# GpSimd's elementwise work to VectorE and ScalarE in a two-layer attention trunk

## The chip, the cores and the metric

The kernel runs on one core of one Trainium2 chip. The metric is the device time of one execution in microseconds (us); the median of several executions is compared. In the profile PE is TensorE (its matmuls), PEld its weight loads, DVE is VectorE, ACT is ScalarE, POOL is GpSimd and SP is SyncE, whose queue issues loads.

## The reference

One batch of 512 tokens of width 1024 goes through two layers, each with a residual and an RMS norm before and after. Layer A is multi-head latent attention (8 heads), layer B differential attention (8 heads); both have a SiLU gate.

```python
def mla_layer(h, ...):                       # layer A
    u = rmsnorm(h, pre_g); c_q, c_kv, k_r, z = split(u @ w_in)
    q = rmsnorm(c_q) @ w_uq                  # per head 128 plain + 64 with rope
    c_kv = rmsnorm(c_kv); k_n, v = c_kv @ w_uk, c_kv @ w_uv
    p = masked_softmax((q_n k_n + rope(q_r) rope(k_r)) * scale)
    return h + rmsnorm(((p v) * silu(z)) @ w_o, post_g)

# the shared K/V of layer B come from h once: k = rope(k), v = u @ w_kv
def diff_layer(h, ...):                      # layer B
    q, z = split(rmsnorm(h) @ w_in); q = rope(q)   # q1, q2 of 64 each
    p = masked_softmax(q1 k1 * scale) - lam * masked_softmax(q2 k2 * scale)
    o = rmsnorm(p v, subln_g) * (1 - lam_init)
    return h + rmsnorm((o * silu(z)) @ w_o, post_g)
```

The mask is chunk-causal: a query block of 128 sees the keys up to its own chunk of 64.

## The kernel before, in words

Every matmul is made of three: each operand is split into a rounded high part and the rest, and `mm3` (L187 to L191) adds high by high, high by low and low by high into PSUM. Activations lie transposed, features on the partitions and the 512 tokens along the row, so most elementwise instructions are 128x512.

**Weights.** `Stream` (L63) holds the weights in their order of use. For each unit SP's queue loads the raw tile `wr` (L89). For the first units `wh` and `wl` are made by VectorE (L104, L107, L137 and L138); from L365 on `ws.cast` is true: the high part `wh` comes by a second, rounding transfer on GpSimd's queue (L112), and VectorE makes `wl` as raw minus high (L113). `ahead` keeps two units ahead of PE, in three buffers.

**Stages.** The start (L336 to L364) runs over eight blocks of x: ScalarE scales x into `xh` (L338) and squares it (L347), VectorE makes `xl` (L339), the squares are added up in `acc_x` (L349), and PE makes five projections `g`. Then `trig` (L320) makes sine and cosine tables, VectorE for the angles (L322 to L328) and ScalarE for the values (L329 to L331); the tables for layer A are `CA` and `SA`, for layer B `CB` and `SB`. `cq` (L391) makes six projections and adds their squares in `acc_q` (L400); `acc_kv` (L413) does so for `g`. Between the second and the third `cq` PE adds `acc_x` and `acc_kv` over the partitions (L421 to L430, tiles `ssx` and `sskv`), which needs their split by ScalarE and VectorE (`axh`, `axl`, `akh`, `akl`).

Layer A then goes through its heads in the order `aorder`, layer B in `border` (L250): projections k, q and z of later heads stand between the scores (s), transposes (t) and the product with v (p) of earlier ones. In layer B `proj_b` makes k and q: PE's projection, `rope` (L375: a shuffle, two products and a sum: L378, L379, L380, L381), ScalarE's halves (L836, L840), and VectorE's rests (L838 for q, L841 for k). `scores_b` is four matmuls for each of four query blocks (L872, L875), then `softmax_part` (L522 on VectorE, L525 on ScalarE); the second softmax, times lambda over its sum, is scaled (L883, tile `ec`) and subtracted (L884, tile `eb`), in four pieces of 128, 256, 384 and 512 columns. `transposes` turns the result on PE and splits it (`pth` on ScalarE, `ptl` on VectorE, L133 and L138). After the product with v, `subln` scales the gate by the head's norm (L910 to L912).

Between the layers `chain_a` (L717) normalises each of four token tiles, stores the rows (L722), and scales them into h (L723); PE transposes h (`trans_h`, L735), and VectorE and ScalarE evacuate it (`evac_h`, L742 to L745). In `vb_half0` (L753) the first projections of layer B, `vb_0` to `vb_3`, stand between the transposes of tiles 2 and 3.

**Order.** A scheduler of the framework decides, when the kernel is built, in which order the instructions stand on each engine, from its own model of their times; each engine then runs its list strictly in order, waiting for semaphores. Only in `wo_end` and `vb_half0` PE's order is that of the program (`pe_order`). So an edit that changes where one operation runs can change the order of others on every engine.

Of the kernel before, what the change touches and what calls it, by code (L numbers as in the profile page):

```python
# [15 lines left out]
AF = mybir.ActivationFunctionType  # L16
ALU = mybir.AluOpType
# [41 lines left out]
def f(ap):  # L59
    return ap.bitcast(F32)  # L60
# [80 lines left out]
def body(tc, ins, outs, dbg=None):  # L141
    nc = tc.nc
    ctx = ExitStack()
    with ctx:
        _body(ctx, tc, nc, ins, outs, dbg or {})


def _body(ctx, tc, nc, ins, out, dbg):
    pool = lambda name, bufs, **k: ctx.enter_context(tc.tile_pool(name=name, bufs=bufs, **k))
# [13 lines left out]
    act, dve, gps, pe = nc.scalar, nc.vector, nc.gpsimd, nc.tensor  # L163

    def ps(name):
        return psp.tile([P, 512], F32, tag="ps", name=name)

    def big_t(name, dt=F32R):
        return big.tile([P, 8, 512], dt, tag="big", name=name)

    def hd_t(name, dt=F32R):
        return hd.tile([P, 512], dt, tag="hd", name=name)

    def tmp_t(name, dt=F32):
        return tmp.tile([P, 512], dt, tag="tmp", name=name)

    def tab_t(name):
        return tmp.tile([P, 512], F32, tag="tmp", name=name)

    def sm_t(name, n=4, bufs=None):  # L180
        return sm.tile([P, n], F32, tag=name, name=name, bufs=bufs)
# [5 lines left out]
    def mm3(o, w, x, first, last):  # L187

        pe.matmul(o, w[0], x[0], start=first, stop=False)  # L189
        pe.matmul(o, w[0], x[1], start=False, stop=False)  # L190
        pe.matmul(o, w[1], x[0], start=False, stop=last)  # L191
# [20 lines left out]
    def add_wo(src):  # L212
        def second(p):
            ws.add(src[1, p], lambda which, k:
                   w1[which][:, 2 * p:2 * p + 2].rearrange("p a b -> p (a b)") if w1 else None)
        for p in range(3):
            ws.add(src[0, p])
            second(p)
        second(3)
        ws.add(src[0, 3])  # L220

    ws = Stream(nc, wrp, whp, wlp)
# [32 lines left out]
    border = [(nm, h) for nm, h in border if h < H]  # L255
    for nm, h in border:
        if nm in "kqz":
            ws.add(ins[f"w_{nm}b"][h], None, None if nm == "q" else ("pool", "pool"))
    add_wo(ins["w_ob"])

    wraw = big_t("wraw", F32).rearrange("p a b -> p (a b)")
# [30 lines left out]
    def col(c):  # L292
        return cols[:, c:c + 1]
# [19 lines left out]
    acc_x = hd_t("acc_x", F32)  # L313
# [22 lines left out]
    for kc in range(KC):  # L336
        for c in first if kc == 0 else [slice(0, 512)]:
            behind = act.activation(xh[:, kc, c], xr[:, kc, c], AF.Copy, scale=col(C_PRE + kc))  # L338
        dve.scalar_tensor_tensor(xl[:, kc], xr[:, kc], col(C_PRE + kc), f(xh[:, kc]),  # L339
                                 op0=ALU.mult, op1=ALU.subtract)  # L340
        g = [ws.get()]
        if kc == 0:
            g.append(ws.get())
        ws.ahead(3 if kc == 0 else 2)
        sq = acc_x if kc == 0 else hd_t("sqx", F32)
        with tc.issue_after(behind.ins):
            act.activation(sq, xr[:, kc], AF.Square)  # L347
        if kc:
            gps.tensor_tensor(acc_x, acc_x, sq, op=ALU.add)  # L349
        for m in range(5):  # L350
            gh, gl = g[1 if kc == 0 and m else 0]
            k = m - 1 if kc == 0 and m else m
            ms = slice(k * P, k * P + P)
            if kc == 0 and m == 0:
                for c in first:
                    pe.matmul(g0[m][:, c], gh[:, 0, ms], xh[:, kc, c], start=c is first[0], stop=False)
                pe.matmul(g0[m], gl[:, 0, ms], xh[:, kc], start=False, stop=False)
                pe.matmul(g0[m], gh[:, 0, ms], xl[:, kc], start=False, stop=False)
                continue
            if m == 4:  # L360
                for part in (xh, xl):
                    pe.matmul(g0[m], gh[:, 0, ms], part[:, kc], start=kc == 0 and part is xh, stop=kc == 7 and part is xl)
                continue
            mm3(g0[m], (gh[:, 0, ms], gl[:, 0, ms]), (xh[:, kc], xl[:, kc]), kc == 0, kc == 7)  # L364
# [10 lines left out]
    def rope(src, C, Sn, shuf):  # L375

        a, b = tmp_t("ra"), tmp_t("rb")
        dve.stream_shuffle(b, src, shuf)  # L378
        dve.tensor_tensor(a, src, C, op=ALU.mult)  # L379
        gps.tensor_tensor(b, b, Sn, op=ALU.mult)  # L380
        dve.tensor_tensor(a, a, b, op=ALU.add)  # L381
        return a

# [4 lines left out]
    acc_q, acc_kv, rx = hd_t("acc_q", F32), hd_t("acc_kv", F32), tab_t("rx")  # L388
    xe_col = sm_t("xe_col", 4, 1)

    def cq(m):  # L391
        wh, wl = ws.get()
        o = ps(f"cq{m}")
        for kc in range(KC):
            mm3(o, (wh[:, kc], wl[:, kc]), (xh[:, kc], xl[:, kc]), kc == 0, kc == KC - 1)
        act.activation(cqh[:, m], o, AF.Copy, scale=col(C_Q + m))
        sq = acc_q if m == 0 else tmp_t("sq")
        act.activation(sq, o, AF.Square)
        if m:
            gps.tensor_tensor(acc_q, acc_q, sq, op=ALU.add)  # L400
        dve.scalar_tensor_tensor(cql[:, m], o, col(C_Q + m), f(cqh[:, m]), op0=ALU.mult, op1=ALU.subtract)
        ws.ahead()

# [5 lines left out]
    for m in range(4):  # L409
        sq = acc_kv if m == 0 else hd_t("sqkv", F32)  # L410
        act.activation(sq, g0[m], AF.Square)
        if m:
            gps.tensor_tensor(acc_kv, acc_kv, sq, op=ALU.add)  # L413
    axh, axl = tmp_t("axh", F32R), tmp_t("axl", F32R)
    split(nc, axh, axl, acc_x)
    akh, akl = hd_t("akh"), hd_t("akl")
    split(nc, akh, akl, acc_kv)
    cq(0)
    cq(1)
    ssx = ps("ssx")  # L420
# [25 lines left out]
    zg = big_t("za", F32)  # L446
# [174 lines left out]
    v3 = lambda a: a.rearrange("p (k t) -> p k t", k=4)  # L621
# [4 lines left out]
    def post(parts, done=None):  # L626

        r = sm_t("r", 1)
        inv_norm(r, [o for o, _, _, _ in parts], [j3(tmp_t("sq"), o) for o, _, _, _ in parts])
        for o, g, _, t in parts:  # L630
            dve.tensor_tensor(t, o, g, op=ALU.mult)
        for n, (_, _, res, t) in enumerate(parts):
            dve.scalar_tensor_tensor(res, t, r, res, op0=ALU.mult, op1=ALU.add)
            if done:
                done(n)
# [79 lines left out]
    def chain_a(i, o1):  # L715
        res = xrows[i]
        ts = [hTf[:, 4 * n:4 * n + 4, i * P:i * P + P] for n in range(2)]  # L717
        post([(v3(o), v3(g), v3(x), t) for o, g, x, t in zip((st["acc"][i], o1), g_a, res, ts)])
        r = sm_t("rh", 1)
        inv_norm(r, [v3(a) for a in res], ts)  # L720
        for n in range(2):
            gps.dma_start(hdr[i, n], res[n])  # L722
            gps.tensor_scalar(ts[n], v3(res[n]), r, 1.0, op0=ALU.mult, op1=ALU.mult)  # L723
        hrows[i] = ts

    gkv_b = cols[:, C_BKV:C_BKV + 8]
# [76 lines left out]
    for p in range(4):  # L803
        wh, wl = ws.get()
        for kc in (2 * p, 2 * p + 1):
            act.activation(hT2h[:, kc], hTf[:, kc], AF.Copy, scale=col(C_BPRE + kc))
            dve.scalar_tensor_tensor(hT2l[:, kc], hTf[:, kc], col(C_BPRE + kc), f(hT2h[:, kc]),
                                     op0=ALU.mult, op1=ALU.subtract)
# [10 lines left out]
    zg = big_t("zb", F32)  # L819
# [41 lines left out]
    def scores_b(h):  # L861
        (kb, kl), (qb, _) = qkb.pop(("k", h)), qkb.pop(("q", h))
        second = {}

        def src(i):


            n = P * (i + 1)
            ti = slice(i * P, i * P + P)
            os = [ps(f"sb{h}_{g}_{i}") for g in range(2)]  # L870
            for g in range(2):
                pe.matmul(os[g][:, :n], qb[g][:, ti], kb[g][:, :n], start=True, stop=False)  # L872
            for g in range(2):
                rs = slice(64 * g, 64 * g + 64)
                pe.matmul(os[g][:, :n], qb[g][rs, ti], kl[rs, :n], start=False, stop=True)  # L875
            second[i] = os[1]
            return os[0]

        (e1, r1), (e2, r2) = softmax_part(h, "bc", [src, second.get], -SCALE_B)
        dve.tensor_scalar(r2, r2, lam_c, None, op0=ALU.mult)  # L880
        for i in range(NT):
            w = slice(OFF[i], OFF[i] + P * (i + 1))
            gps.tensor_scalar(e2[:, w], e2[:, w], r2[:, i:i + 1], 1.0, op0=ALU.mult, op1=ALU.mult)  # L883
            dve.scalar_tensor_tensor(e1[:, w], e1[:, w], r1[:, i:i + 1], e2[:, w],  # L884
                                     op0=ALU.mult, op1=ALU.subtract)
        es[h] = e1
# [19 lines left out]
    def subln(h):  # L906
        b = ps(f"ssb{h}")
        pe.matmul(b, ones_r if h < H - 1 else ones, ob.pop(h), start=True, stop=True)
        rs = tmp_t("rs")
        act.activation(rs, b, AF.Ln, bias=eps_c, scale=1.0 / 128)  # L910
        act.activation(rs, rs, AF.Exp, scale=-0.5)
        (dve if h > 4 else gps).tensor_tensor(zg[:, h], zg[:, h], rs, op=ALU.mult)  # L912

    def after_b(h, o):
        subln_sq(h, o)
# [101 lines left out]
```

## Time and profile before

| | us |
|---|---|
| median of 3 executions | 608.12 (607.16 to 609.12) |
| the profiled execution | 609.05 |
| its span in the trace | 607.0 |
| PE busy | 589.6 |
| DVE busy | 420.1 |
| ACT busy | 255.0 |
| POOL busy | 158.8 |

The span is what the trace covers; the execution's own time is 2.05 us longer. Busy times of engines overlap. PE's share is 97% of the span, so what PE does not do in the span is 17.4 us; a part of its busy time is at half clock. A row of a timeline gives the start, the duration, the engine, the line, what is written and read, and in brackets for how long the engine had been idle and what ended that.

### The profile page before, as it was taken

What the parts mean: (1) busy time and instruction counts of PE and PEld (TensorE: products, weight loads), DVE (VectorE), ACT (ScalarE), POOL (GpSimd) and SP (SyncE); (2) the same over time, 40 slices, a digit from 0 to 9 for tenths busy, and PEclk for the clock granted to TensorE, in tenths of its full rate; (3) what the DMA queues carried; (4) which work ended last, traced back from release to release, by engine and by line L of the source; (5) the groups of instructions that cost most, each with busy time, mean ns of one, the idle gap of its engine ahead of it and who ended that gap; (6) DMA issues with size and microseconds to landing.
All of it is one profiled execution on the core that took longest, in us unless ns stands there. A gap on an engine that the chain in (4) does not pass through costs nothing.

```text
span 607.0 us, 7782 instructions
## 1 busy us (share of the span) xinstructions
PE 589.6 (97%) x2742; PEld 481.4 (79%) x2742; DVE 420.1 (69%) x806; ACT 255.0 (42%) x560; POOL 158.8 (26%) x216
## 2 busy tenths in 40 slices
PE   7999999999999999999999999999997999999995
PEld 6786888888888888888888887878776677687885
DVE  6997852345576666756876458847999688988654
ACT  6046311122334444421664125245664539647431
POOL 5232610112232323321440112405325134242000
PEclk9998999999999999999999999999999699799999
DMA  8155555555552426787431656464244142269302
GB/s 305 43 157 191 157 190 208 183 164 140 170 147 91 135 91 207 239 326 268 165 106 47 245 174 202 138 209 138 83 129 137 52 157 76 99 194 357 110 35 105
DMA packets 32215, 96.61 MB, mean 159 GB/s; under 512 B 3760, under 2 KB 4400, under 8 KB 32176
## 3 DMA queue, kind: packets, MB, share of 16 engines
q1 hardware_dynamic: 19296, 53.51, 25.8%
q0 software_dynamic: 12736, 42.47, 22.7%
q8 instruction: 22, 0.36, 0.3%
q10 hardware_dynamic: 144, 0.13, 0.1%
q14 instruction: 17, 0.14, 0.1%
HBM read 91.90 MB, written 4.19 MB: 158 GB/s over the span
## 4 chain that ended last, share of the span: by engine, by line
PE 79%; DVE 10%; ACT 3%; DMA 3%; issue 3%; POOL 1%; SPq 1%; DVEq 0%; POOLq 0%
PE wo L189 5%; PE wo L190 5%; PE wo L191 5%; PE sb L872 3%; PE qb L189 3%; PE za L189 2%; PE vb L189 2%; PE za L191 2%; PE vb L191 2%; PE vb L190 2%; PE za L190 2%; PE sb L875 2%; PE qb L190 2%; PE qb L191 2%; PE pt L563 2%
## 5 line engine op out<-in xcount | busy, mean ns | idle before, releaser
L113 DVE TENSOR_TENSOR wl<-wr,wh 128x1024 fp32r<-128x1024 f32 (+2 forms) x74 | 84.2, 1137 | 81.5 <-issue 20.1
L133 ACT ACTIVATE pth<-pt 128x512 fp32r<-128x512 f32 (+1 forms) x48 | 22.1, 528 | 28.5 <-PE pt L563 26.9
L138 DVE TENSOR_TENSOR ptl<-pt,pth 128x512 fp32r<-128x512 f32 (+1 forms) x48 | 26.7, 591 | 2.1 <-ACT pth L133 1.9
L883 POOL TENSOR_SCALAR ec<-ec,ric 128x128 f32<-128x128 f32 (+3 forms) x32 | 23.7, 753 | 16.9 <-DVE ric L880 15.8
L189 PE MATMUL qb<-hT2h,wh 128*128 128x512 f32 x64 | 27.7, 433 | 0.0
L551 POOL TENSOR_SCALAR ea<-ea,ria 128x128 f32<-128x128 f32 (+3 forms) x32 | 16.9, 540 | 41.0 <-DVE ria L528 40.9
L872 PE MATMUL sb<-k,q 128*128 128x128 f32 (+3 forms) x64 | 22.7, 404 | 4.7 <-DVE q L838 4.7
L525 ACT ACTIVATE ea<-ea,mxa 128x128 f32<-128x128 f32 (+3 forms) x32 | 17.9, 561 | 22.2 <-DVE mxa L522 22.1
L189 PE MATMUL wo<-w1h,ogh 128*128 128x512 f32 (+1 forms) x72 | 26.7, 371 | 0.0
L190 PE MATMUL qb<-hT2l,wh 128*128 128x512 f32 x64 | 26.5, 415 | 0.0
L190 PE MATMUL wo<-w1l,ogh 128*128 128x512 f32 (+1 forms) x72 | 26.4, 367 | 0.0
L191 PE MATMUL qb<-hT2h,wl 128*128 128x512 f32 x64 | 26.4, 412 | 0.0
L191 PE MATMUL wo<-w1h,ogl 128*128 128x512 f32 (+1 forms) x72 | 26.4, 366 | 0.0
L380 POOL TENSOR_TENSOR rb<-rb,SB 128x512 f32<-128x512 f32 x16 | 20.5, 1282 | 21.9 <-DVE rb L378 19.7
L189 PE MATMUL kb<-hT1h,wh 128*128 128x512 f32 x64 | 25.3, 396 | 0.0
L190 PE MATMUL wo<-wl,ogh 128*128 128x512 f32 x64 | 25.2, 393 | 0.0
L189 PE MATMUL za<-xh,wh 128*128 128x512 f32 x64 | 25.0, 391 | 0.0
L189 PE MATMUL zb<-hT2h,wh 128*128 128x512 f32 x64 | 25.0, 390 | 0.0
L191 PE MATMUL kb<-hT1h,wl 128*128 128x512 f32 x64 | 25.0, 390 | 0.0
L190 PE MATMUL kb<-hT1l,wh 128*128 128x512 f32 x64 | 24.9, 390 | 0.0
L191 PE MATMUL zb<-hT2h,wl 128*128 128x512 f32 x64 | 24.9, 390 | 0.0
L191 PE MATMUL za<-xh,wl 128*128 128x512 f32 x64 | 24.9, 389 | 0.0
(341 smaller groups left out, 1787.1 us busy)
## 6 DMA issues: line engine op xcount, KB each, us to landing
wr<-in_w_za SPq DMA_DIRECT2D x8, 512.0 KB, 4.0
wh<-in_w_za POOLq DMA_DIRECT2D x8, 512.0 KB, 4.5
wr<-in_w_oa SPq DMA_DIRECT2D x8, 512.0 KB, 4.5
wr<-in_w_vb SPq DMA_DIRECT2D x8, 512.0 KB, 4.1
wr<-in_w_kb SPq DMA_DIRECT2D x8, 512.0 KB, 4.0
wh<-in_w_kb POOLq DMA_DIRECT2D x8, 512.0 KB, 3.8
wr<-in_w_qb SPq DMA_DIRECT2D x8, 512.0 KB, 3.5
wh<-in_w_qb POOLq DMA_DIRECT2D x8, 512.0 KB, 4.4
```

What stands on the lines that cost most here:

```text
L113: self.nc.vector.tensor_tensor(lo, raw, f(hi), op=ALU.subtract)
L133: nc.scalar.activation(hi, src, AF.Copy)
L138: (nc.vector if lo_eng == "dve" else nc.gpsimd).tensor_tensor(lo, src, f(hi), op=ALU.subtract)
L189: pe.matmul(o, w[0], x[0], start=first, stop=False)
L190: pe.matmul(o, w[0], x[1], start=False, stop=False)
L191: pe.matmul(o, w[1], x[0], start=False, stop=last)
L380: gps.tensor_tensor(b, b, Sn, op=ALU.mult)
L525: act.activation(ev, ev, AF.Exp, bias=mx[:, one], scale=-1.0, accum_out=l[:, one])
L551: gps.tensor_scalar(ev, ev, ri[:, i:i + 1], 1.0, op0=ALU.mult, op1=ALU.mult)
L563: pe.transpose(t[:, o + (i - j) * P:o + (i - j) * P + P], e[:, OFF[i] + j * P:OFF[i] + j * P + P], ident)
L872: pe.matmul(os[g][:, :n], qb[g][:, ti], kb[g][:, :n], start=True, stop=False)
L883: gps.tensor_scalar(e2[:, w], e2[:, w], r2[:, i:i + 1], 1.0, op0=ALU.mult, op1=ALU.mult)
```

## The change

Six lines move an operation from GpSimd to another engine, with the same operands:

- L349, L400, L413: the sums `acc_x` (7), `acc_q` (5) and `acc_kv` (3), to VectorE
- L380: rope's second product (21: 16 in layer B, 5 in layer A), to VectorE
- L912: the gate times the head's norm, for heads 0 to 4 (5), to VectorE, where heads 5 to 7 had it
- L723: the scaling of h (8), to ScalarE
- L883: the scaling of the second softmax in layer B (32), to ScalarE

The seventh, at L258, no longer names GpSimd as the engine that splits the k and z weights of layer B. GpSimd keeps the rounding transfers (L112), the stores of the rows (L722) and layer A's scaling (L551).

```diff
@@ -255,7 +255,7 @@
-            ws.add(ins[f"w_{nm}b"][h], None, None if nm == "q" else ("pool", "pool"))
+            ws.add(ins[f"w_{nm}b"][h])
@@ -346,7 +346,7 @@
-            gps.tensor_tensor(acc_x, acc_x, sq, op=ALU.add)
+            dve.tensor_tensor(acc_x, acc_x, sq, op=ALU.add)
@@ -377,7 +377,7 @@
-        gps.tensor_tensor(b, b, Sn, op=ALU.mult)
+        dve.tensor_tensor(b, b, Sn, op=ALU.mult)
@@ -397,7 +397,7 @@
-            gps.tensor_tensor(acc_q, acc_q, sq, op=ALU.add)
+            dve.tensor_tensor(acc_q, acc_q, sq, op=ALU.add)
@@ -410,7 +410,7 @@
-            gps.tensor_tensor(acc_kv, acc_kv, sq, op=ALU.add)
+            dve.tensor_tensor(acc_kv, acc_kv, sq, op=ALU.add)
@@ -720,7 +720,7 @@
-            gps.tensor_scalar(ts[n], v3(res[n]), r, 1.0, op0=ALU.mult, op1=ALU.mult)
+            act.activation(ts[n], v3(res[n]), AF.Copy, scale=r)
@@ -880,7 +880,7 @@
-            gps.tensor_scalar(e2[:, w], e2[:, w], r2[:, i:i + 1], 1.0, op0=ALU.mult, op1=ALU.mult)
+            act.activation(e2[:, w], e2[:, w], AF.Copy, scale=r2[:, i:i + 1])
@@ -909,7 +909,7 @@
-        (dve if h > 4 else gps).tensor_tensor(zg[:, h], zg[:, h], rs, op=ALU.mult)
+        dve.tensor_tensor(zg[:, h], zg[:, h], rs, op=ALU.mult)
```

The scheduler's order changes with it in many places. Three of them, and one told in words, are spoken of below.

On VectorE, where head 4's q is made (`qb_3971`; its two halves are `q_4002` and `q_4003`; `eb_3912` is the softmax of head 3, `wl_4078` a weight's low part), before:

```order
L138 TENSOR_TENSOR ptl_4028<-pt_1_4015,pth_4027 128x512
L884 SCALAR_TENSOR_TENSOR eb_3912<-eb_3912,rib,ec_3913 128x384
L884 SCALAR_TENSOR_TENSOR eb_3912<-eb_3912,rib,ec_3913 128x512
L113 TENSOR_TENSOR wl_4078<-wr_4008,wh_4077 128x1024
L381 TENSOR_TENSOR ra<-ra,rb 128x512
L378 STREAM_SHUFFLE rb<-kb_4035 128x512
L379 TENSOR_TENSOR ra<-kb_4035,CB 128x512
L838 TENSOR_TENSOR q_4002<-ra,q_4002 64x512
L838 TENSOR_TENSOR q_4003<-ra,q_4003 64x512
```

and with the change:

```order
L880 TENSOR_SCALAR ric<-ric,ls 128x4
L113 TENSOR_TENSOR wl_4078<-wr_4008,wh_4077 128x1024
L381 TENSOR_TENSOR ra<-ra,rb 128x512
L884 SCALAR_TENSOR_TENSOR eb_3912<-eb_3912,rib,ec_3913 128x128
L884 SCALAR_TENSOR_TENSOR eb_3912<-eb_3912,rib,ec_3913 128x256
L884 SCALAR_TENSOR_TENSOR eb_3912<-eb_3912,rib,ec_3913 128x384
L378 STREAM_SHUFFLE rb<-kb_4035 128x512
L379 TENSOR_TENSOR ra<-kb_4035,CB 128x512
L884 SCALAR_TENSOR_TENSOR eb_3912<-eb_3912,rib,ec_3913 128x512
L838 TENSOR_TENSOR q_4002<-ra,q_4002 64x512
L380 TENSOR_TENSOR rb<-rb,SB 128x512
L838 TENSOR_TENSOR q_4003<-ra,q_4003 64x512
```

Rope's sum (L381), on which ScalarE's halves of q wait, moved from behind the four subtractions of L884 to ahead of them; rope's product for k (L380) now stands between the two halves of q, and the product for q some rows ahead of this piece.

On ScalarE, between the layers, where PE's projection `vb_0` is evacuated into `vhb` (`xr_2421` and `xr_2422` are the rows of token tile 2, whose transposes are PE's next work behind `vb_0`), before:

```order
L306 ACTIVATE r<-r 128x1
L133 ACTIVATE hT1h<-hg 128x4x128 x2
L614 ACTIVATE hTf,ss<-xr_2425 128x4x128
L614 ACTIVATE hTf,ss<-xr_2426 128x4x128
L133 ACTIVATE vhb<-vb_0_2755 128x512
L742 ACTIVATE hTf<-hT_0_2782 128x4x128
```

and with the change:

```order
L305 ACTIVATE rh<-v_2647 128x1
L305 ACTIVATE r<-v_2713 128x1
L306 ACTIVATE rh<-rh 128x1
L306 ACTIVATE r<-r 128x1
L133 ACTIVATE vhb<-vb_0_2755 128x512
L723 ACTIVATE hTf<-xr_2421,rh 128x4x128
L723 ACTIVATE hTf<-xr_2422,rh 128x4x128
L614 ACTIVATE hTf,ss<-xr_2425 128x4x128
```

The two scalings of tile 2 (L723) now stand on ScalarE, behind the evacuation of `vb_0`.

On VectorE, where head 6's q is made (`qb_4399`; halves `q_4430` and `q_4431`), before:

```order
L381 TENSOR_TENSOR ra<-ra,rb 128x512
L884 SCALAR_TENSOR_TENSOR eb_4340<-eb_4340,rib,ec_4341 128x128
L138 TENSOR_TENSOR ptl_4456<-pt_0_4442,pth_4455 128x512
L138 TENSOR_TENSOR ptl_4456<-pt_2_4444,pth_4455 128x256
L884 SCALAR_TENSOR_TENSOR eb_4340<-eb_4340,rib,ec_4341 128x256
L113 TENSOR_TENSOR wl_4506<-wr_4436,wh_4505 128x1024
L138 TENSOR_TENSOR ptl_4456<-pt_1_4443,pth_4455 128x512
L884 SCALAR_TENSOR_TENSOR eb_4340<-eb_4340,rib,ec_4341 128x384
L838 TENSOR_TENSOR q_4430<-ra,q_4430 64x512
L884 SCALAR_TENSOR_TENSOR eb_4340<-eb_4340,rib,ec_4341 128x512
L838 TENSOR_TENSOR q_4431<-ra,q_4431 64x512
```

and with the change:

```order
L381 TENSOR_TENSOR ra<-ra,rb 128x512
L880 TENSOR_SCALAR ric<-ric,ls 128x4
L900 TENSOR_TENSOR sqs<-sqo,sqs 64x512
L138 TENSOR_TENSOR ptl_4456<-pt_0_4442,pth_4455 128x512
L113 TENSOR_TENSOR wl_4506<-wr_4436,wh_4505 128x1024
L138 TENSOR_TENSOR ptl_4456<-pt_2_4444,pth_4455 128x256
L138 TENSOR_TENSOR ptl_4456<-pt_1_4443,pth_4455 128x512
L838 TENSOR_TENSOR q_4430<-ra,q_4430 64x512
L838 TENSOR_TENSOR q_4431<-ra,q_4431 64x512
L884 SCALAR_TENSOR_TENSOR eb_4340<-eb_4340,rib,ec_4341 128x128
L884 SCALAR_TENSOR_TENSOR eb_4340<-eb_4340,rib,ec_4341 128x256
```

The halves of q moved ahead of all four subtractions of L884.

At the start, on VectorE, the low part of the weight of the second `cq` (`wl_489`, L113) moved from behind the last L328 of the angles for layer B to ahead of the last three L327 before it.

## Rows read from the trace of the kernel before

**Rows 1.** The page, part 1: busy us (share of span) xinstructions, each engine.

```profile
PE 589.6 (97%) x2742; PEld 481.4 (79%) x2742; DVE 420.1 (69%) x806; ACT 255.0 (42%) x560; POOL 158.8 (26%) x216
```

**Rows 2.** Waits of PE: tile and line <- releaser: us in total, times, longest.

```profile
PE sb L872 <- DVE q L838: 4.7, 4, 2.5
```

**Rows 3.** Stretches: length, busy us (x instructions) per engine, PEclk, DMA share, GB/s.

```profile
49.60:53.00 3.40, 3.37 (x8) 2.69 (x9) 3.29 (x5) 1.74 (x4) 2.02 (x1) 0.50 0.38 92
...
464.90:469.40 4.50, 1.02 (x4) 0.74 (x4) 4.41 (x5) 2.75 (x5) 2.89 (x2) 1.00 0.54 195
469.40:479.70 10.30, 10.30 (x24) 6.32 (x24) 8.08 (x24) 7.61 (x21) 0.00 (x0) 0.50 0.18 51
...
512.00:517.20 5.20, 4.60 (x23) 3.53 (x21) 5.14 (x9) 3.71 (x7) 1.87 (x4) 1.00 0.39 118
517.20:520.60 3.40, 2.54 (x12) 1.52 (x11) 3.34 (x9) 1.69 (x5) 1.83 (x2) 1.00 0.34 135
520.60:527.40 6.80, 6.80 (x15) 4.42 (x15) 6.80 (x20) 6.16 (x17) 1.13 (x1) 0.50 0.25 78
...
8.00:17.50 9.50, 6.28 (x25) 4.06 (x23) 9.47 (x7) 7.21 (x12) 8.68 (x7) 1.00 0.96 366
450.00:475.00 25.00, 21.50 (x89) 15.74 (x88) 24.42 (x51) 16.44 (x43) 8.13 (x10) 0.89 0.31 91
```

**Rows 4.** PE in order of time, head 4's first scores: start, us, what, [idle <-releaser].

```profile
467.35 0.30 PE L872 MATMUL sb<-k,q 128*128 128x128 f32 x1 [2.47 <-DVE q L838]
...
468.94 0.33 PE L872 MATMUL sb<-k,q 128*128 128x128 f32 x1 [1.03 <-DVE q L838]
```

**Rows 5.** VectorE in order of time, the same stretch.

```profile
465.90 2.98 DVE L838 TENSOR_TENSOR q<-ra,q 64x512 fp32r<-64x512 f32 x2
```

**Rows 6.** GpSimd in order of time, the same stretch.

```profile
465.40 1.26 POOL L380 TENSOR_TENSOR rb<-rb,SB 128x512 f32<-128x512 f32 x1 [1.94 <-DVE rb L378]
466.70 1.63 POOL L912 TENSOR_TENSOR zb<-zb,rs 128x512 f32<-128x512 f32 x1
```

**Rows 7.** Instruction groups with moved work: busy us, mean ns | idle, releaser.

```profile
L883 POOL TENSOR_SCALAR ec<-ec,ric 128x128 f32<-128x128 f32 (+3 forms) x32 | 23.7, 753 | 16.9 <-DVE ric L880 15.8
...
L525 ACT ACTIVATE ea<-ea,mxa 128x128 f32<-128x128 f32 (+3 forms) x32 | 17.9, 561 | 22.2 <-DVE mxa L522 22.1
...
L723 POOL TENSOR_SCALAR hTf<-xr,rh 128x512 f32<-128x512 f32 x8 | 8.0, 1012 | 10.1 <-DVE r L310 6.8 <-DVE rh L310 3.3
...
L133 ACT ACTIVATE vhb<-vb 128x512 fp32r<-128x512 f32 x8 | 4.8, 594 | 26.0 <-PE vb L191 26.0
...
L912 DVE TENSOR_TENSOR zb<-zb,rs x3: 678/691/693, 562.1 to 578.0; 128x512 f32<-128x512 f32 x3
```

**Rows 8.** The page, part 6: transfers, KB each, median us from issue to landing.

```profile
wh<-in_w_za POOLq DMA_DIRECT2D x8, 512.0 KB, 4.5
```

**Rows 9.** VectorE in order of time at the start, the last step of layer B's angles.

```profile
41.81 1.40 DVE L328 TENSOR_SCALAR ang<-ang 128x512 f32<-128x512 f32 x1
```

**Rows 10.** PE in order of time, from the first cq to the third.

```profile
35.46 0.39 PE L189 MATMUL cq<-xh,wh 128*128 128x512 f32 x1
...
40.90 0.39 PE L189 MATMUL cq<-xh,wh 128*128 128x512 f32 x1
...
47.15 0.50 PE L421 MATMUL ssx<-axh,ones_r 128*128 128x512 f32 x1 [0.65 <-ACT axh L133]
...
49.63 0.79 PE L189 MATMUL cq<-xh,wh 128*128 128x512 f32 x1 [0.17 <-DVE cql L401]
```

**Rows 11.** PE in order of time, the transposes of h behind vb_0.

```profile
311.21 1.15 PE L735 MATMUL hT<-ident,hTf 128*128 128x128 f32 x8
```

**Rows 12.** VectorE in order of time, head 6's q halves.

```profile
515.84 0.68 DVE L838 TENSOR_TENSOR q<-ra,q 64x512 fp32r<-64x512 f32 x1
516.55 0.75 DVE L884 SCALAR_TENSOR_TENSOR eb<-eb,rib,ec 128x512 f32<-128x512 f32 x1
517.34 0.69 DVE L838 TENSOR_TENSOR q<-ra,q 64x512 fp32r<-64x512 f32 x1
```

## The prediction

> **What bounds the kernel now.** I read the busy times first: PE works 589.6 of the 607.0 us, VectorE 420.1, ScalarE 255.0, GpSimd 158.8 [rows 1]. So PE bounds the kernel, and no change here gives PE less to do. Time can come only from the 17.4 us in which PE stands still and from stretches in which it runs at half clock. The waits of PE come second: scores wait 4.7 us for VectorE's rests of q, at four heads [rows 2]. Third, the stretches. The granted clock falls from 2.4 to 1.2 GHz (PEclk 1.00 to 0.50) at 49.6 for 3.4 us, at 469.4 for 10.3 and at 520.6 for 6.8 [rows 3]; half of each is lost, 1.7, 5.1 and 3.4 us. Each follows a stretch in which PE stood still among few or narrow products; at 8 to 17.5 PE was busy for only 6.28 of 9.50 us, in waits among full-width projections for what VectorE and ScalarE prepare, and the clock stayed at 1.00 [rows 3].
>
> Then the place of the longest wait. Head 4's first two scores wait 2.47 and 1.03 us for L838 [rows 4]. VectorE is not idle there: it is busy 4.41 of 4.50 us [rows 3], and the two L838 alone take 2.98 us [rows 5], while at head 6 the same instruction takes 0.68 and 0.69 [rows 12]. What differs is GpSimd: during the first pair it runs L380 for 1.26 us and L912 for 1.63 us [rows 6], during the second pair nothing. So GpSimd's products stretch VectorE's instructions, and in 450 to 475 VectorE is busy 24.42 of 25.00 us [rows 3].
>
> **The change part by part.** *What VectorE gets.* 7 + 21 + 5 + 3 + 5 = 41 instructions of 128x512. The three L912 that it runs already take 0.69 us each [rows 7], so 41 x 0.69 = 28.3 us. *What it gets back.* GpSimd's rival work goes; from the pair above, 2.98 - 2 x 0.69 = 1.6 us for 2.9 us of GpSimd work. Over the run both are of like size, so VectorE's load hardly changes; only places count.
>
> *What ScalarE gets.* 32 scalings L883. On GpSimd they take 0.753 us on average; ScalarE's exponentials of the same four sizes take 0.561 [rows 7]. So 32 x 0.56 = 18 us, and 2.2 us per head in place of 3.0. Eight L723 go from 1.012 us to about the 0.594 of an evacuation of 128x512 [rows 7], 4.8 us. ScalarE was busy 255.0 us, and 16.44 of 25 in the densest stretch, so it takes 2.2 more per head; it pays only where one of them stands ahead of something that PE waits for.
>
> *L258* does nothing: layer B's weights are split after L365, where the rounding transfer is used and the engine's name is never read. GpSimd's queue is left with transfers and L551, so transfers that stood behind sums go out earlier; their buffers come free with PE's progress, and I count nothing for it.
>
> *The start.* Gain: if the waits of 8 to 17.5 go, PE's loop over x ends 9.50 - 6.28 = 3.2 us sooner [rows 3], at 32.3 in place of 35.46, where the first `cq` begins [rows 10]. But PE then waits longer at `ssx`: in the new order `wl_489` stands ahead of the last three L327, and its transfer goes out when the first `cq` is done, 5.4 us later (35.46 to 40.90 [rows 10]), at 37.7; it lands 4.5 us later [rows 8], at 42.2. The five instructions from L113 to L328 at about 0.69 make 45.7, against 41.81 + 1.40 = 43.2 before [rows 9]. From there to `ssx` it was 47.15 - 43.2 = 3.9 us [rows 10], all ScalarE: 49.6 now. Behind `ssx` the third `cq` came after 2.48 us [rows 10], with waits for splits that are now ready; four products take about 1.0. So 50.6 against 49.63, **+1.0**. Bounds: -1.1, if all 3.2 us reach the third `cq` less 2.1 for three more sums, and +2.1, if nothing is gained at the start and those are paid. I keep the half clock that follows as it is.
>
> *h, tile 2.* PE's transposes began at 311.21, right behind the last product of `vb_0` and with no wait [rows 11]. GpSimd scaled the tile beforehand. ScalarE now first evacuates `vb_0`, which is PE's own last work, and then scales. A product lasts 0.39 us [rows 10] and the next begins before its end, so `vb_0` is done some 0.2 after 311.2; with 0.59 for `vhb`, 0.59 for the first L723 and two handovers of 0.06 (468.88 to 468.94 at head 4 [rows 4, 5]) PE waits **+1.5**. Half clock behind it is bounded by nothing (the start, with 3.2 us of waits) and 3.4 (the stretch behind head 6). The neighbours are full-width projections, as at the start; I take nothing.
>
> *Head 2's q.* The four waits sum to 4.7; less 2.47, 1.03 and head 6's 0.86 that leaves 0.3, which an L838 of 0.69 ends: **-0.3**.
>
> *Head 4's q.* The first half is ready when it was: rope's sum comes sooner, but four L884, a shuffle and a product now stand between it and L838. The pair with k's L380 between takes 3 x 0.67 = 2.0 in place of 2.98: **-1.0**. The half clock of 10.3 us follows a stall of 3.5 us; with 2.5 left I keep it whole (bounds 0 and -5.1).
>
> *Head 6's q.* The halves are ready at 516.5 and 518.0, with an L884 between them [rows 12]; they now stand ahead of all four, so they come some 2 us sooner and PE doesn't wait. It stood still 0.60 us in 512 to 517.2 and 0.86 in 517.2 to 520.6 [rows 3]: **-1.5**. The half clock of 6.8 us behind it goes: **-3.4**.
>
> Layer A and the end have no place where PE waits for a moved instruction; GpSimd's L551 there is untouched, and I count nothing.
>
> Sum: +1.0 + 1.5 - 0.3 - 1.0 - 1.5 - 3.4 = -3.7. The profiled execution took 609.05, so 605.35; it stood 0.93 above the median of 608.12. Forecast **604.4 us**.
>
> **A rule that speaks against it.** The trace has VectorE at 98% in 450 to 475 [rows 3], and the change adds work to it there. The Trainium skill, "Perfetto Trace Analysis", section "Optimizing Scalar/DVE Operations", advises the opposite move when VectorE is saturated: off to ScalarE or even GpSimd. It adds that the last may not help, as the two share a port. By the rule alone the sum would be the slower rival below. The trace bears out the addition: L838 beside GpSimd's products, 2.98 for two, against 0.68 and 0.69 [rows 5, 6, 12].
>
> **The rivals.**
> 1. *Larger gain, about 597.8.* Head 4's stall shrinks below what the clock answers to, -5.1, and tile 2's scaling finds ScalarE early, -1.5. For: the halves were late by GpSimd's work alone. Against: the stall that I work out is still 2.5 us.
> 2. *No change, about 608.8.* Head 6's scores lose the wait, but another of that stage (a weight's low part, `ptl`) puts the clock down as before, +3.4, and head 4's pair gains nothing because what is saved is spent on L380, +1.0. For: 28.3 us come onto VectorE. Against: at head 6 the order itself has changed.
> 3. *VectorE becomes the bound in layer B, about 616.6.* Every head adds two L380 and one L912, about 2.0 us, to a list that PE waits for at heads 2, 4 and 6. If VectorE's instructions do not get shorter, the 6.2 us of gains there (0.3 + 1.0 + 1.5 + 3.4) fall away and 3 x 2.0 comes on top: 604.4 + 12.2 = 616.6. It decides where relief per head is under 2.0 us. For: 24.42 of 25 us. Against: one pair alone shows relief of 1.6. This is what the page's rule would do here.
>
> **How the numbers follow.** Forecast 0.47 (its own range 600 to 608: head 4's clock and the bounds of the start), rival 1 0.16, rival 2 0.17, rival 3 0.20. A measurement of this kernel can tell about 0.3%, 1.8 us, from no change. Faster means below 606.3: rival 1 and most of the forecast, 0.58. Same, to 609.9: rival 2 and some of the forecast, 0.20. Slower: rival 3 and the start's and tile 2's upper bounds, 0.22. The range 597 to 612.5 leaves out the better half of rival 1 and most of rival 3.
>
> **What would show it.** L838 at 0.69 us throughout layer B; head 6's scores without a wait and no half clock behind it; a new wait of about 1.5 us before the transposes of tile 2, ended by L723; a wait of several us at `ssx` while the early waits are gone; a wait of about 2.5 us at head 4 with its half clock. I am wrong if VectorE's instructions stay long with GpSimd quiet, if new half-clock stretches stand at heads that had none, or if layer A has changed.

## The result and the profile after

| | us | against before, 95% interval |
|---|---|---|
| before, median of 4 runs | 608.62 (607.16 to 614.71) | |
| after, median of 4 runs | 616.32 (615.45 to 619.03) | 1.0117 [1.0070, 1.0164] |
| after, the profiled execution | 616.61 | |
| its span | 614.7 (before 607.0) | |

The change makes the kernel 1.2% slower. 604.4 us was forecast; 616.3 is above the range. The page's busy times of after, which answer to [rows 1]:

```profile
PE 591.9 (96%) x2742; PEld 484.7 (79%) x2742; DVE 420.2 (68%) x847; ACT 273.8 (45%) x600; POOL 67.3 (11%) x135
```

VectorE has 41 more instructions and the same busy time, 420.2 against 420.1 us; so the ones that it had became shorter, in sum, by what the new ones take. PE, with the same 2742 matmuls, is busy 2.3 us longer and stands still for 614.7 - 591.9 = 22.8 us in place of 17.4. The waits of PE (engine, tile and line, what it waited for; us in total, times, longest):

```profile
PE ssx L421 <- issue: 6.2, 1, 6.2
PE sb L872 <- DVE q L838: 4.0, 4, 2.0
PE qb L189 <- DVE mxb L522: 1.5, 1, 1.5
PE mtok L459 <- DVE acc_q L443: 1.4, 1, 1.4
PE hT L735 <- ACT hTf L723: 1.3, 1, 1.3
PE o L190 <- DVE ptl L138: 1.2, 1, 1.2
```

Besides the line of [rows 2], the kernel before had two that bear on these:

```profile
PE ssx L421 <- ACT axh L133: 0.7, 1, 0.7
PE o L190 <- DVE ptl L138: 0.5, 1, 0.5
```

So five of the lines of after are new or longer, each a wait at one place (that for `ptl` is at another place than before). And while PE works there are now five stretches at 1.2 GHz (the last column but two is PEclk; the busy times before it are those of PE, its loads, DVE, ACT and POOL):

```profile
46.60:53.40 6.80, 5.30 (x13) 4.17 (x14) 3.48 (x5) 1.87 (x3) 0.00 (x0) 0.50 0.25 77
87.60:91.00 3.40, 3.40 (x10) 2.64 (x9) 1.83 (x5) 1.29 (x2) 0.00 (x0) 0.50 0.58 186
384.60:388.00 3.40, 3.38 (x8) 2.70 (x9) 3.40 (x15) 3.40 (x13) 0.00 (x0) 0.50 0.35 137
476.70:486.90 10.20, 10.20 (x24) 6.26 (x24) 8.68 (x25) 7.82 (x21) 0.00 (x0) 0.50 0.17 51
551.80:558.60 6.80, 6.80 (x14) 4.04 (x15) 6.46 (x21) 6.26 (x20) 0.00 (x0) 0.50 1.07 403
```

The first and the fourth answer to two of [rows 3]; head 6's has gone; those at 87.6, 384.6 and 551.8 stand behind new waits: `mtok`, the second q, head 7.

**Where the 7.7 us come from.** The start of the same matmul in the two timelines, and how far after is behind at it:

| matmul | before | after | behind |
|---|---|---|---|
| first `cq` | 35.46 | 30.90 | -4.6 |
| `ssx` | 47.15 | 48.10 | +0.9 |
| third `cq` | 49.63 | 49.51 | -0.1 |
| first `za` | 73.11 | 73.45 | +0.3 |
| `mtok` | 83.99 | 85.87 | +1.9 |
| first `va` | 117.58 | 121.17 | +3.6 |
| transposes of tile 2 | 311.21 | 317.26 | +6.1 |
| head 2's k | 382.46 | 391.76 | +9.3 |
| head 4's first scores | 467.35 | 474.75 | +7.4 |
| head 6's first scores | 516.67 | 522.40 | +5.7 |
| z behind head 7's q | 531.59 | 533.89 | +2.3 |
| head 7's first scores | 544.68 | 549.12 | +4.4 |
| last matmul | 600.45 | 608.15 | +7.7 |

PE's own list changed too, above all in the projections `g` at the start, in some heads of layer A and in both output projections, but not at `mtok`, the second q and head 7. Between `va` and the transposes head 5 of layer A adds 1.2. The steps of the prediction stand at the start, tile 2, and heads 2, 4 and 6, and together give some -5 us. Four places that it did not name, `mtok`, head 5 of layer A, the second q and head 7, give some +13.

**The four places, on VectorE** (start, us, engine, line, what is written and read, in brackets the idle time before and what ended it). `mtok`, which PE waits 1.38 us for:

```profile
83.99 1.23 DVE L113 TENSOR_TENSOR wl<-wr,wh 128x1024 fp32r<-128x1024 f32 x1 [1.72 <-DMA wh<-in_w_za]
85.14 0.68 DVE L443 SCALAR_TENSOR_TENSOR acc_q<-acc_x,acc_q 128x512 f32<-128x512 f32 x1
```

L443 is what `mtok` reads. In the new order the low part of a z weight (`wl_748`) stands ahead of it, and that one waits 1.72 us for its rounding transfer. Before, L443 stood two such low parts earlier:

```profile
77.58 0.68 DVE L443 SCALAR_TENSOR_TENSOR acc_q<-acc_x,acc_q 128x512 f32<-128x512 f32 x1
```

There too VectorE then stood idle in front of a low part, for 3.29 us until 83.29, but behind L443. Head 5 of layer A:

```profile
250.19 3.09 DVE L138 TENSOR_TENSOR ogl<-za,ogh 128x512 fp32r<-128x512 f32 x5
253.20 1.61 DVE L138 TENSOR_TENSOR ptl<-pt,pth 128x512 fp32r<-128x512 f32 x3
```

`ptl` belongs to the product that PE wants next; five rests of the gated output stand ahead of it, and the first product that reads such a rest begins only at 256.41. Before, `ptl` went first:

```profile
248.00 1.58 DVE L138 TENSOR_TENSOR ptl<-pt,pth 128x512 fp32r<-128x512 f32 x3
```

The second q:

```profile
381.70 1.23 DVE L113 TENSOR_TENSOR wl<-wr,wh 128x1024 fp32r<-128x1024 f32 x1 [3.33 <-DMA wh<-in_w_kb]
382.84 1.40 DVE L841 TENSOR_TENSOR kl<-ra,k 64x512 fp32r<-64x512 f32 x2
384.27 0.29 DVE L522 CUSTOM_DVE_ANT_0 eb<-sb,mask 128x128 f32<-128x128 f32 x1
```

This piece of the list is the same before and after. PE's next q projection waits for the maxima (L522), which read the scores; they stand behind the low part, and that waits 3.33 us for its transfer. In the kernel before it waited 0.21:

```profile
372.60 1.23 DVE L113 TENSOR_TENSOR wl<-wr,wh 128x1024 fp32r<-128x1024 f32 x1 [0.21 <-DMA wh<-in_w_kb]
```

GpSimd issued that transfer at 373.93 in after, as far behind before as PE is (367.77 there). The view of the transfers gives its time to landing, in after and then in the kernel before:

```profile
wh<-in_w_kb POOLq DMA_DIRECT2D x1, 512.0 KB, 7.7
```

```profile
wh<-in_w_kb POOLq DMA_DIRECT2D x1, 512.0 KB, 4.8
```

And head 7:

```profile
545.28 1.23 DVE L113 TENSOR_TENSOR wl<-wr,wh 128x1024 fp32r<-128x1024 f32 x1 [2.68 <-PE ssb L908]
546.42 1.93 DVE L884 SCALAR_TENSOR_TENSOR eb<-eb,rib,ec 128x128 f32<-128x128 f32 x4
548.39 1.40 DVE L838 TENSOR_TENSOR q<-ra,q 64x512 fp32r<-64x512 f32 x2
```

VectorE stands still for 2.68 us in front of a low part (`wl_4856`), with all four subtractions and head 7's q behind it. Before, q and the subtractions stood ahead of that low part, the first half of q at

```profile
539.06 1.07 DVE L838 TENSOR_TENSOR q<-ra,q 64x512 fp32r<-64x512 f32 x1
```

In after PE's scores wait 2.00 us, and 6.8 us at half clock follow.

At three of the four places VectorE was idle shortly before PE's wait, for longer than that wait: 1.72 us against 1.38, 3.33 against 1.49, 2.68 against 2.00. It wasn't short of time; what PE needed stood in line behind an instruction that could not start.

### The profile page after: what moved, and what is told of

It reads as the page before. It is cut to its first block, busy times and chain, and to the rows that moved or that the text cites. A ratio compares the mean times of both kernels' runs of the same rounds, so it can differ in the third digit from the quotient of the medians.

```text
span 614.7 us, 7730 instructions
## 1 busy us (share of the span) xinstructions
PE 591.9 (96%) x2742; PEld 484.7 (79%) x2742; DVE 420.2 (68%) x847; ACT 273.8 (45%) x600; POOL 67.3 (11%) x135
## 4 chain that ended last, share of the span: by engine, by line
PE 65%; issue 20%; DVE 7%; DMA 4%; POOL 1%; ACT 1%; SPq 1%; POOLq 0%; DVEq 0%; ACTq 0%
PE wo L189 5%; PE wo L190 5%; PE wo L191 5%; PE sb L872 2%; PE pt L563 2%; PE qb L189 2%; PE za L189 2%; PE za L190 2%; DMA wh<-in_w_kb 2%; PE sb L875 2%; PE za L191 2%; PE zb L190 2%; PE zb L191 2%; PE zb L189 2%; PE qb L190 2%
## 5 line engine op out<-in xcount | busy, mean ns | idle before, releaser
L113 DVE TENSOR_TENSOR wl<-wr,wh 128x1024 fp32r<-128x1024 f32 (+2 forms) x74 | 83.0, 1122 | 80.6 <-issue 17.5
L190 PE MATMUL za<-xl,wh 128*128 128x512 f32 x64 | 25.6, 400 | 0.0
L191 PE MATMUL wo<-wh,ogl 128*128 128x512 f32 x64 | 25.6, 400 | 0.0
L189 PE MATMUL wo<-wh,ogh 128*128 128x512 f32 x64 | 25.1, 405 | 0.0
```

Of the source, the lines that this page charges most:

```text
L113: self.nc.vector.tensor_tensor(lo, raw, f(hi), op=ALU.subtract)
```

## The experiments

**Theory O (order).** The engines' new work is harmless; the time is lost to the lists that the scheduler makes of it. **Theory L (load).** The instructions that VectorE and ScalarE got are themselves what PE waits for, and a list in another order would only move the wait.

Most experiments hold the order at some place. The program numbers its instructions as the code makes them, alike in both kernels, and a list of numbers becomes edges that say only "issue behind this one on the same engine", with no wait and no data:

```diff
+ORDER = ["685 65", ...]          # first number, then steps
+def pin(tc, nc):
+    by = {i.name: i for i in nc.cur_bb.bb.instructions}
+    info = mybir.DependencyInfo(mybir.DependencyClass.NoSync, mybir.DependencyReason.DATA)
+    for text in ORDER:
+        n, last = 0, None
+        for step in text.split():
+            n += int(step)
+            i = by.get(f"I-{n}")
+            if i is not None and (last is None or i.engine == last.engine):
+                if last is not None:
+                    tc.add_manual_dep(i, last.name, info, reason="issue_after")
+                last = i
 ...
         body(tc, ins, out, dd)
+        pin(tc, nc)
```

Each ratio below is against runs of the kernel before on the same chip; the median of these was 608.6 to 615.1 us, so ratios are compared and not microseconds. PE's, GpSimd's and SyncE's lists are the scheduler's in every run: "order" below means the held lists and what the scheduler makes of the others with them.

**1. The changed kernel in the old order.** ORDER is the whole list of VectorE and of ScalarE as the kernel before has it; the moved instructions, which are not in those lists, fall where the scheduler puts them.

> The changed kernel, every operation on its new engine, but on VectorE and ScalarE all instructions that did not move are held to the order that they had before the change; the scheduler places only the moved ones. Theory O (the time is lost to the new order: at four places an instruction that PE waits for now stands behind a weight's low part that itself waits for a transfer or a buffer, or behind other work): the new waits at mtok, at head 5 of layer A and at head 7 of layer B go, what GpSimd cost VectorE stays gone, so 599 to 607 us. Theory L (the 41 instructions on VectorE and 40 on ScalarE are themselves too much in the tight places): 612 us or more.

Measured: 602.82 us, ratio 0.9896 [0.9861, 0.9931]. Its waits of PE:

```profile
PE sb L872 <- DVE q L838: 2.8, 2, 1.9
PE o L190 <- DVE ptl L138: 1.6, 2, 1.2
...
PE sa L191 <- DVE qnl L138: 1.0, 1, 1.0
PE ssx L421 <- issue: 1.0, 1, 1.0
PE qb L189 <- DVE mxb L522: 0.6, 1, 0.6
```

(The profiled execution is the longest of seven, 607.33 us.) The waits at `mtok`, head 5 and head 7 are gone, and that at `ssx` is 1.0 in place of 6.2. Some come back elsewhere, as L has it: the `o` waits shown are at 175.6 and 570.6, the `qnl` wait is at 178.4, and 3.4 us at half clock follow it. But the same work on the same engines is 1.0% faster than before in the one order and 1.2% slower in the other. L, which asked for 612 us or more, falls. The transfer for the second k was late here too (6.8 us), so it comes late in the old order too; PE's wait for what stands behind it is 0.6 here.

**2. The old engines in the new order.** The kernel before with the lists of after.

> The kernel before, every operation on its old engine, but VectorE and ScalarE held to the order of the changed kernel, less the moved ones. Theory O: the waits of the new order appear with no added instruction, at mtok, head 5 of layer A and head 7, so 613 to 621 us. Theory L: nothing was added, so about the time of before, 606 to 611 us.

Measured: 629.11 us, ratio 1.0319 [1.0278, 1.0360], slower than either theory gave, and so outside O's range too. Waits of PE:

```profile
PE ssx L421 <- issue: 7.4, 1, 7.4
PE sb L872 <- DVE q L838: 5.7, 3, 3.5
PE mtok L459 <- DVE acc_q L443: 3.5, 1, 3.5
PE g L191 <- DVE sp L107: 2.7, 1, 2.7
```

The new order is worse still with GpSimd at work, with `mtok` and `g` waiting longer and the longest L838 at 1.76 us. With runs 1 and 2 the table is whole:

| | old order | new order |
|---|---|---|
| old engines | 1 (before) | 1.0319 |
| new engines | 0.9896 | 1.0117 (after) |

The engines give 1.0% in the old order and 1.0117 / 1.0319 = 2.0% in the new; the order costs 3.2% with the old engines and 1.0117 / 0.9896 = 2.2% with the new. The change made both moves at once.

**3. Four holds in the changed kernel.** L443 ahead of the low part; the three `ptl` of head 5 ahead of the five `ogl`; tile 2's L723 ahead of `vhb`; head 7's q ahead of its low part.

```diff
+ORDER = ["685 65", "2120 4 -2 86 2 2 2 2", "2658 2 120", "4630 2 226"]
```

> The changed kernel with four places held in another order: acc_q's last step ahead of the weight's low part that waits for its transfer, head 5's ptl ahead of the five ogl, tile 2's scaling ahead of the evacuation of vb_0, head 7's halves of q ahead of the weight's low part that waits for a buffer. Theory O: 1.5 and its half clock 1.6, 1.2, some 0.9, 2.1 and its half clock 3.3 go: 616 less 10.6 is 605 to 608 us. Theory L: the same amount of work, so the waits come back as other waits and 613 to 618 us stay.

Measured: 602.82 us, ratio 0.9882 [0.9839, 0.9925]. Waits of PE:

```profile
PE ssx L421 <- issue: 6.3, 1, 6.3
PE qb L189 <- DVE mxb L522: 1.9, 1, 1.9
...
PE hT L735 <- ACT hTf L723: 1.4, 1, 1.4
```

Three of the four waits are gone, and a handful of edges turn 1.2% slower into 1.2% faster. That is more than O gave (605 to 608 us); the profiled execution, the longest of nine at 607.02 us, has 9.5 us less of span than after, near what the table of starts gives for the three places (9.9); where the median gains more is not shown. The hold at head 5 also moved products in PE's own list. The hold on L723 did nothing: in its place ScalarE shows

```profile
312.14 1.34 ACT L723 ACTIVATE hTf<-xr,rh 128x512 f32<-128x512 f32 x2 [0.88 <-DVE rh L310]
```

so the scaling, now ahead of `vhb`, waits for the norm of its own tile, which comes late too.

**4, 5 and 6. Holds one at a time.** Only `mtok` ("685 65"):

> The changed kernel with one hold alone: acc_q's last step (L443) ahead of the weight's low part that waits for its transfer. Theory O: the wait before mtok (1.4 us) and the half clock behind it (3.4 us long, 1.7 lost) go and nothing else, so about 613 us (611.5 to 614.5). Theory L: no gain, 615 to 618 us.

Measured: 616.15 us, ratio 1.0111 [1.0049, 1.0172]; a miss for O, in L's range. At its own place the hold worked: the wait has gone and the first `va` comes 3.0 us sooner than in after, head 2's k 5.5 us sooner, as the wait at the second q is shorter too (0.8). Then it is lost again, in stretches at half clock (columns as above):

```profile
426.00:429.40 3.40, 3.40 (x15) 1.96 (x14) 3.37 (x11) 2.07 (x6) 0.00 (x0) 1.00 0.58 177
429.40:436.20 6.80, 6.80 (x15) 4.70 (x15) 5.94 (x16) 5.49 (x14) 0.00 (x0) 0.50 0.29 77
548.90:559.10 10.20, 10.20 (x23) 6.19 (x24) 9.69 (x26) 8.49 (x21) 0.00 (x0) 0.50 0.97 344
```

The second of these has no counterpart in after, nor has a further one at 525.0 for 3.4 us; the third is 3.4 us longer than its counterpart. Only head 7 ("4630 2 226"):

> The changed kernel with one hold alone: head 7's halves of q (L838) ahead of the weight's low part that waits for its buffer. Theory O: the wait of 2.0 us before head 7's scores and the half clock behind it (6.8 us long, 3.4 lost) go, so about 611 us (609 to 613). Theory L: no gain, 615 to 618 us.

Measured: 610.09 us, ratio 0.9987 [0.9944, 1.0030]: 1.3% less than after's ratio, at least what the table of starts has at head 7 (2.1 + 3.3 us, 0.9%). Only the second q, whose low part is held behind the maxima:

```diff
+ORDER = ["3292 -47"]
```

> The changed kernel with one hold alone: the weight's low part whose transfer landed 7.7 us after its issue (L113 before the first scores) stands behind the maxima of those scores (L522). Theory O: VectorE no longer stands in front of a late transfer, the wait of 1.5 us before the second q and its half clock (3.4 us long, 1.7 lost) go, 612 to 614 us, and up to 4 us more or less from half-clock stretches that fall elsewhere. Theory L: 615 to 618 us.

Measured: 614.84 us, ratio 1.0050 [1.0002, 1.0098]. The wait and its half clock are gone and PE reaches head 3's k about 3.0 us sooner, as the table has it (1.5 of wait and 1.7 of half clock); the profiled span is 611.6 against 614.7. The interval overlaps that of after, so the gain is read from the trace and not from the times.

**7. Only the start in the old order.** VectorE's and ScalarE's lists up to `mtok` as before, free from there on.

> The changed kernel with the old order of VectorE and ScalarE up to mtok alone. Theory O: the 6.2 us before ssx become about 1, as in the first experiment's kernel (ssx at 42.8 in place of 48.1), and mtok's 1.4 us and its half clock go: 616 less 5.3 less 3.1 is 607 to 609 us. Theory L: 613 us or more.

Measured: 604.73 us, ratio 0.9886 [0.9849, 0.9923]. PE at `ssx`, which began at 48.10 in after:

```profile
42.85 0.47 PE L421 MATMUL ssx<-axh,ones_r 128*128 128x512 f32 x1 [0.84 <-issue]
```

The order of the start, up to `mtok`, is worth most of what was held by itself: 5.3 us at `ssx`, and with the wait at `mtok` and both early half-clock stretches gone 9.5 us at the first `va`. This is the gain that the prediction saw in the start's early waits, 4.6 us at the first `cq`, and then saw eaten up by the weight's low part ahead of the last angles. It need not be eaten. The time lies below O's range of 607 to 609 us; part of the reason is that the wait at the second q is missing from this trace (its transfer landed after 5.0 us).

**8. Only L723 back on GpSimd.** The one line of the diff reverted.

> The changed kernel with the eight scalings L723 back on GpSimd. The step of the prediction that held in the trace (ScalarE evacuates vb_0 before it scales tile 2, PE waits 1.3 us) would be worth 1.4 us and no half clock: 614 to 616 us. If it is worth nothing because the scaling on GpSimd is as late: 616 to 617 us.

Measured: 614.89 us, ratio 1.0056 [1.0025, 1.0087]. The wait for tile 2 has gone and PE gains 1.45 us there, though GpSimd is only just in time:

```profile
314.26 2.74 POOL L723 TENSOR_SCALAR hTf<-xr,rh 128x512 f32<-128x512 f32 x2 [4.47 <-DVE r L310]
```

The transposes begin at 316.55, and those that read the second half, done at 317.00, at 317.05. The time of the run is no measure of this place alone: in its trace the transfer for the second k landed after 3.8 us, so that wait is missing too, and the half clock behind head 7 is 10.2 us long in place of 6.8.

**9. Which group carries the gain?** The changed kernel in the old order (as run 1), with one group of moved work given back to GpSimd: L883; or the sums (L349, L400, L413); or rope's products and L912. Theory C: the gain is contention's end, so each group that returns takes back its share. Theory R: it is rope's products alone.

> The first experiment's kernel (new engines, old order, 602.8 us) with the 32 scalings L883 back on GpSimd. If each operation that leaves GpSimd gives VectorE its own time back (theory C, contention), L884 and L838 beside L883 are long again, some 1 us per head at heads where PE waits: 604 to 608 us. If only rope's products matter (theory R): within 1 us of 602.8.

> The first experiment's kernel (602.8 us) with the 15 sums L349, L400 and L413 back on GpSimd. Theory C: the start's waits of 3.2 us in 8 to 17.5 come back and ssx begins some 4 us later: 606 to 608.5 us. Theory R: within 1 us of 602.8.

> The first experiment's kernel (602.8 us) with rope's 21 products L380 and the five L912 back on GpSimd. Theory C: at heads 2, 4 and 6 L838 is long again beside them, but VectorE has 26 instructions less: 602 to 606 us. Theory R: the gain in layer B was theirs, 606 to 609 us.

| on GpSimd again | us | ratio | longest L838 |
|---|---|---|---|
| none (run 1) | 602.82 | 0.9896 [0.9861, 0.9931] | 0.69 |
| L883 | 605.67 | 0.9874 [0.9810, 0.9938] | 1.07 |
| sums | 608.13 | 0.9893 [0.9824, 0.9962] | 0.69 |
| rope's products and L912 | 603.22 | 0.9819 [0.9764, 0.9874] | 1.65 |

(On the chip of the last three the kernel before took 615.11 us, so the ratios are to be read; the microseconds, which lie in C's ranges, were expected against another chip's 602.8.) The four intervals overlap: the times don't tell which group carries the gain, and neither theory is borne out by them. What the profiles tell is local. With rope's products back, VectorE and GpSimd at head 4:

```profile
458.87 3.04 DVE L838 TENSOR_TENSOR q<-ra,q 64x512 fp32r<-64x512 f32 x2
```

```profile
458.43 1.26 POOL L380 TENSOR_TENSOR rb<-rb,SB 128x512 f32<-128x512 f32 x1 [1.59 <-ACT q L836]
459.66 1.70 POOL L912 TENSOR_TENSOR zb<-zb,rs 128x512 f32<-128x512 f32 x1
```

The pair of L838 takes 3.04 us, for 2.98 in [rows 5], beside the same two GpSimd products as in [rows 6]; in after every one of the 16 is at 0.69 (the row of L838: least, median and longest ns, then the first and last start):

```profile
L838 DVE TENSOR_TENSOR q<-ra,q x16: 684/686/689, 374.3 to 549.1; 64x512 fp32r<-64x512 f32 x16
```

With the sums back, the first `cq` starts at 34.75 in place of 30.73, and `g` waits for VectorE's splits again: beside the sums, VectorE's rounding of a 128x576 weight (L104) takes up to 1.55 us, and in run 1 at most 0.46. So each group's contention is real where it stands; how much of it PE feels is not told by these times.

**10. What the runs point to.** The changed kernel with L723 on GpSimd, the old order up to `mtok`, and the holds at head 5, the second q and head 7.

```diff
-            act.activation(ts[n], v3(res[n]), AF.Copy, scale=r)
+            gps.tensor_scalar(ts[n], v3(res[n]), r, 1.0, op0=ALU.mult, op1=ALU.mult)
 ...
+ORDER = [..., "2120 4 -2 86 2 2 2 2", "3292 -47", "4630 2 226"]
```

> The changed kernel with L723 back on GpSimd, the old order of VectorE and ScalarE up to mtok (so that ssx does not wait 6 us), the holds of head 5 and head 7, and the weight's low part of head 2's k behind the first scores' maxima. Theory O: against the kernel with four holds (602.8) the start gains some 4, tile 2's wait 1.4 and the wait at the second q (1.9 and its half clock) in the runs where it stands: 595 to 600 us. Theory L: what is taken out of one place comes back in the next, 602 to 606 us.

Measured: 596.98 us, ratio 0.9803 [0.9767, 0.9838], faster than both kernels. Busy times and the waits of PE:

```profile
PE 583.5 (98%) x2742; PEld 479.4 (81%) x2742; DVE 420.2 (71%) x847; ACT 270.1 (45%) x592; POOL 75.2 (13%) x143
```

```profile
PE ssx L421 <- issue: 0.8, 1, 0.8
PE hT L735 <- POOL hTf L723: 0.4, 1, 0.4
```

VectorE's load is that of after to the tenth, 420.2 us; PE stands still for 11.0 us in place of 22.8, and while it works two stretches at half clock are left (463.6 for 6.8 us and 511.4 for 3.4) in place of five.

## Why the prediction was wrong

**What held.** VectorE's load: "hardly changes" was 420.1 to 420.2, and L838 is at 0.69 throughout layer B. The start, +1.0 forecast at the third `cq`, was -0.1 there and +0.3 at the first `za`; the half clock, which the prediction kept as it was, is 6.8 us long in place of 3.4, but begins while PE stands still and lasts only 0.4 us longer (to 53.4). The chain was the one worked out: early waits gone (-4.6 at the first `cq`, 3.2 forecast), then 6.2 us at `ssx`, behind the low part (40.38), the three L327, L328 (done at 44.12), ScalarE's sine and cosine tables and, as before the change, a load of ScalarE's own function table ahead of `axh`, which `ssx` reads:

```profile
46.07 1.28 ACT L318 ACT_TABLE_LOAD   x1
```

Tile 2, +1.5, was +1.44 and ended by L723, as the rows on ScalarE show (that GpSimd had scaled the tile beforehand holds for the first half; the second was done at 311.65, while the transposes ran):

```profile
316.00 0.60 ACT L133 ACTIVATE vhb<-vb 128x512 fp32r<-128x512 f32 x1 [0.97 <-PE vb L191]
316.49 1.32 ACT L723 ACTIVATE hTf<-xr,rh 128x512 f32<-128x512 f32 x2
```

Head 2 was -0.3 as forecast; head 4's two waits, 2.47 and 1.03, became 0.88 and 0.86, -1.8 for -1.0, its half clock kept; head 6's waits and half clock, -1.5 and -3.4, were -4.9 together. The named terms sum to -3.7 in the prediction and to about -5.3 in the trace.

**The step that failed** is the sentence "Layer A and the end have no place where PE waits for a moved instruction", which put at nothing `mtok` and head 5 of layer A, 4.4 us, and with it the rule behind the whole sum, that only places where PE waited before, or where a moved instruction stands, can change: by it the second q and head 7 in layer B, 8.6 us, have no term at all. The new waits end in instructions that did not move between engines (L443, `ptl`, L522, L838) and stand where PE did not wait: `mtok` 1.6 and 1.6 of half clock behind it, head 5 of layer A 1.2, the second q 1.6 and 1.6, head 7 2.1 and 3.3, some 13 us. Experiments 3 to 6 took each of these waits away and left the moved work where it is. Three of the four could be seen in the change's order without a run, though not their size: at `mtok` and head 7 a weight's low part, and at head 5 five `ogl`, went ahead of the instruction that PE needs. The fourth, at the second q, could not: the order there is the same, and what was late was a transfer; that the change made it late is not shown, so these 3.2 us may not be the change's own. Two of the prediction's signs of being wrong came: half clock behind the second q and at head 7, which had none, and a changed layer A.

**The rivals.** Rival 2 named a weight's low part as a new wait with half clock behind it, but at head 6's stage, where it did not come. Rival 3 has the right number, 616.6, by luck. Its 2.0 us a head counts an L912 at every head, while before the first one stood at 448.9, behind head 2's place. And its mechanism asked for VectorE's instructions to stay long; they got short, its waits at heads 2, 4 and 6 shrank, and VectorE stood idle in front of the low parts for 1.72, 3.33 and 2.68 us. A time that comes out as a rival gave it does not show the rival's mechanism: run 1, with the same 41 instructions on VectorE, is faster than before. The Trainium skill, "Perfetto Trace Analysis", section "Optimizing Scalar/DVE Operations", says that offloading some work may make sense if VectorE is saturated; here it was busy 68% of the span and idle in front of the low parts, so the loss does not come from that. Its addition, that VectorE and GpSimd share a port, agrees with the 3.04 against 1.40 us for the pair of L838.

**The clock** multiplied what was missed. Of the 13 us, 1.6 + 1.6 + 3.3 = 6.5 are stretches at 1.2 GHz behind new waits. The prediction had priced half clock only for stretches that were there, and had taken none behind tile 2, where none came.

## What to carry to other kernels

Under a scheduler, an edit that changes engines is an edit of order: go through each engine's new list for an instruction that can wait (for a transfer or a buffer) and now stands ahead of one that TensorE needs, also where nothing waited before. To tell load from order, time the new engines in the old order and the old engines in the new; where order is to blame, a few held pairs can bring the gain back. Whether one engine slows another can be read from two rows of the same instruction, one beside the other engine's work and one without.

## What the runs showed of the hardware

- TensorE's clock fell without a standstill just before it: in the run that holds `mtok` alone, PE is recorded as busy for all of 426.0 to 429.4 at 1.00, in scores of 128 to 512 columns, and at 0.50 from 429.4 on. The same heads kept the full clock in after. So a gain of some us at one place can be lost at another. Executions of one and the same kernel differ by as much: the seven that hold the second q alone took 611.4 to 616.7 us at mean granted clocks of 0.971 to 0.979. Whether single holds add up is therefore not shown: alone, `mtok` gave 0.1% and head 7 1.3%, the four holds together 2.4%, with intervals of 0.4 to 0.6% either way.
- The transfer for the second k landed 7.7 us after its issue in after, and late in six more of the runs (6.5 to 8.1), but after 3.8 to 5.7 in the others and in before. In all seven late cases a fetch of instructions began 0.1 to 0.7 us after the issue, but it did so too in five runs where the transfer landed after 3.9 to 5.7 us. The cause is open and was not tried by itself.
- Also open: which group of moved work carries the gain of run 1, and why the scheduler puts the low parts ahead; its model of the times was not looked at.
